# A hybrid recurrent trunk: 21 pairs of projections by seven products ahead of alternating mixers

## The chip, the cores and the metric

The kernel runs on one core of a Trainium2 chip. The metric is the device time of one execution in microseconds. Before the change it is 2498.74 us, the median of three runs (2498.58 to 2500.35). The engines are TensorE (PE, with its weight loads as PEld), VectorE (DVE), ScalarE (ACT), GpSimd (POOL) and SyncE (SP), which only issues DMAs here.

## The reference

One layer over 1024 frames of 1024 channels, all in float32:

```
h = rmsnorm(x, norm1_g)
q, f, i, g | qk, v, if, o | z, xbc, dt | gate = split(h @ w_in)
HGRN2 (8 heads of 128):  y_hg = rmsnorm(scan(silu(q), log forget(f), i)) * silu(g)
mLSTM (4 heads of 128/256): qk = silu(causal_conv4(qk)); y_ml = rmsnorm(scan(qk, v, if)) * sigmoid(o)
Mamba-2 (4 groups):  xBC = silu(causal_conv4(xbc)); y_mb = rmsnorm((scan(xBC, dt) + d*x) * silu(z))
x = x + (sum_b sigmoid(gate_b) * (y_b @ w_br_b)) @ w_out
x = x + (silu(u_g) * u_v) @ w_down,   u = causal_conv3(rmsnorm(x, norm2_g) @ w_up)
out = rmsnorm(x, final_g)
```

The columns of `w_in` come in blocks of 128. The ones that matter here: `w_hg` (forget, query and output gate of each HGRN2 head), `w_ml` (query, key and two output gates of each mLSTM head), `w_mb` (two x blocks, B and C of each Mamba group), `w_gate` (24 blocks of branch gates) and `w_v` (values in token order, in pairs of blocks).

## The kernel before

Channels lie on the 128 partitions and the 1024 frames along the free axis; `h` is kept in two halves of 512 frames, each as a high and a low part in a rounded 32-bit format. Each weight block is loaded on SP's queue into one of four raw buffers (`weight_`, L106 to 113), split into a high part by ACT (L99) and a low part by DVE (L100), and multiplied in three combinations (high by high, high by low, low by high). A plain block (`gemm`, L136) is 8 x 3 x 2 = 48 matmuls of 512 columns into one of two wide PSUM buffers (`ps_g`). A value pair (`gemm_tok`, L274) is 192 matmuls of 256 columns.

A pair of blocks can also be made by seven half-sized products instead of eight (`pair_gemm`, L171): 7 x 4 x 3 = 84 matmuls for two blocks. For it four sums of quarters of `h` are kept as high and low parts (`sums`, tile `t`, eight buffers), and per pair the weights are combined by four subtractions on DVE (L160) and split again; the products are joined by ACT copies (L188, L191) and DVE additions (L183). Its PE order is fixed as written.

Elsewhere a planner orders each engine's instructions from a model of their times: it takes them in the order of the program as far as they are ready, and weight loads with a higher priority. Tiles rotate through a fixed number of buffers (`BUFS`): `v`, `q`, `k`, `b` and `z` have two, `ta` four, `kT`, `C`, `qe` and `num` one, the outer `gate` three.

The stages: `first` makes `h` from the norm (its two halves), and begins the forget and query blocks and the values of the first heads on the half that is ready; the normed halves are also stored to `h_d`. Then come eight HGRN2 heads (three plain blocks each, and a value pair for every two heads; six levels of small products, L468, between DVE and ACT work), the scalars of mLSTM and Mamba after the sixth head (one block, then a long row of small operations, some of it by way of DRAM, `rows`), four mLSTM heads (four plain blocks, a value pair), and four Mamba groups (four plain blocks with a four-tap convolution each, a value pair). After all mixers: four branch gates as plain blocks, beside them the sums from `h_d` fetched again, 16 branch gates as eight pairs, and four plain gates. All branch gates and the mixers' outputs are stored to DRAM from POOL's queue (`keep`) and fetched on SP's (`fetch`) by the branch products, and the output projection and the MLP follow, the latter with 19 pairs of its own.

Of the kernel before, what the change touches and what calls it, by code (L numbers as in the profile page):

```python
# [18 lines left out]
P = 128  # L19
# [28 lines left out]
class Trunk:  # L48
# [266 lines left out]
    def first(self, hp, early):  # L315

        nc, tc, ins = self.nc, self.tc, self.ins
        self.h = [[hp.tile([P, KT, HALF], F32R, name=f"h{hf}{part}", align_bytes=ALIGN) for part in range(2)]
                  for hf in range(2)]
        with tc.tile_pool(name="n1", bufs=2, side="left", reuse_waits="tile") as pool:  # L320
            xs = [pool.tile([P, KT, HALF], F32, name="n_x") for _ in range(2)]
            tmp = lambda: pool.tile([P, HALF], F32, name="n_t", bufs=6)
# [23 lines left out]
            vw = [self.weight_(ins["w_v"][i], [pool.tile([P, 1024], F32R, name=n, align_bytes=ALIGN) for n in ("w_hi", "w_lo")])  # L346
                  for i in range(2)]
# [11 lines left out]
        mp = early()  # L359
        v = mp.tile([P, NC_, 256], F32, name="v")  # L360
        for i, p in enumerate(pv):
            nc.scalar.copy(out=v[:, 2 * i:2 * i + 2], in_=p)
        return mp, begun, v
# [20 lines left out]
    def hg_v(self, mp, pair):  # L384
        v = mp.tile([P, NC_, 256], F32, name="v")

# [5 lines left out]
    def hg_head(self, mp, hd, v, begun=None):  # L392
# [4 lines left out]
        ps = begun[0] if begun else self.gemm(wb[3 * hd], self.rhs_h)  # L397
        f = mp.tile([P, T], F32, name="ta")
        nc.scalar.activation(out=f, in_=ps, func=AF.Sigmoid)
        ps = begun[1] if begun else self.gemm(wb[3 * hd + 1], self.rhs_h)  # L400
# [213 lines left out]
    def ml_head(self, mp, hd):  # L614
# [108 lines left out]
    def mb_group(self, mp, g):  # L723
# [4 lines left out]
        def channel(j, blk, name):  # L728
            ps = self.gemm(wb[4 * g + j], self.rhs_h)
            t = mp.tile([P, T], F32, name=name)  # L730
# [115 lines left out]

    def gate_pairs(self, pool, some):
        for i in self.in_order(some):
            cs = [pool.tile([P, T], F32, name="c", bufs=3) for _ in range(2)]
            self.pair_gemm(pool, [self.ins["w_gate"][i + j] for j in range(2)], cs)  # L850
            for j in range(2):
                self.gate_end(i + j, cs[j])
# [183 lines left out]
GATES = 4  # L1036
PLAIN = 3
# [109 lines left out]
def build(tc, ins, outs, dbg=None):  # L1147
    stages = dbg or dict(hg=8, ml=4, mb=4, rest=True)
    left = dict(side="left", reuse_waits="tile")
    right = dict(side="right", reuse_waits="tile")  # L1150
    with ExitStack() as ctx:
# [3 lines left out]
        t.h_d = t.dr.tile([2, P, KT, HALF], F32, name="h_dram")  # L1155
# [3 lines left out]
        with tc.tile_pool(name="gp", bufs=3, **right) as t.gp:  # L1159
            with tc.tile_pool(name="hp", bufs=1, **right) as hp:  # L1160
                with ExitStack() as ms:
                    late = ms.enter_context(tc.tile_pool(name="late", bufs=1, **right))
                    early = lambda: Mix(ms.enter_context(tc.tile_pool(name="early", bufs=1, **right)), late)
                    mp, begun, v = t.first(hp, early)
                    t.late_consts(late)
                    t.hg_setup()
                    for hd in range(stages["hg"]):
                        if hd and hd % 2 == 0:
                            v = t.hg_v(mp, hd // 2)
                        t.hg_head(mp, hd, v, begun if hd == 0 else None)  # L1170
                        if hd == 5:
                            t.scalars(mp)
                    for hd in range(stages["ml"]):
                        t.ml_head(mp, hd)
                    for g in range(stages["mb"]):
                        t.mb_group(mp, g)
                if not stages["rest"]:
                    return
                t.gates(range(GATES))
                with tc.tile_pool(name="tp", bufs=1, **right) as tp:  # L1180
                    with tc.tile_pool(name="hx", bufs=2, **left) as hx:
                        xs = [hx.tile([P, KT, HALF], F32, name="h_x") for _ in range(2)]
                        for ks, hf in itertools.product((slice(0, KT // 2), slice(KT // 2, KT)), range(2)):
                            t.fetch(xs[hf][:, ks], t.h_d[hf][:, ks])
                        quarter = lambda hf, k0: [[t.h[hf][part][:, k0 + k] for k in range(KT // 2)] for part in range(2)]
# [63 lines left out]
```

## Time and profile before

| | |
|---|---|
| median of three runs | 2498.74 us |
| the profiled execution | 2498.8 us |
| its span | 2497.0 us |
| mean granted clock, share of full | 0.994 |
| PE / PEld busy | 99% / 85% of the span |
| DVE / ACT / POOL busy | 60% / 40% / 2% |
| moved by DMA | 228.63 MB, mean 92 GB/s |

Busy time of PE is modelled from starts of pipelined matmuls, so the distance between starts is what one costs, not its mean duration. A stretch of the span is given by its start and end in us, and the busy time of each engine in it can be set against its length: where PE is busy throughout, another engine's work is hidden.

### The profile page before, as it was taken

The page shows a single profiled execution, that of the slowest core. Times are in us where ns is not written, and L with a number is a line of the kernel's source. Part 1 is how long each engine was busy: PE and PEld are TensorE (multiplying, and loading weights), DVE is VectorE, ACT ScalarE, POOL GpSimd, SP SyncE. Part 2 cuts the span into 40 slices and gives each one's busy share as a digit, 9 for nine tenths or more (in the row PEclk, how much of TensorE's full clock was granted, in tenths as well). Part 3 has the DMA queues.
Part 4 walks back from the last instruction along what each step waited for, and adds up shares of the span by engine and source line. Part 5 has one row for each costly group of instructions (what it writes and reads, how often), then busy time and mean ns, then how long its engine had stood idle before and what let it go on. Part 6 is the DMA issues. An engine that isn't in the chain of part 4 may idle for free.

```text
span 2497.0 us, 31129 instructions
## 1 busy us (share of the span) xinstructions
PE 2464.3 (99%) x12980; PEld 2116.6 (85%) x12980; DVE 1508.2 (60%) x1888; ACT 1005.8 (40%) x1233; POOL 62.2 (2%) x99
## 2 busy tenths in 40 slices
PE   8999999999999999999999999999999999999998
PEld 6898989889988898998888888888878888878886
DVE  6576767873443366756765323354687887875445
ACT  4444445553433263555444312122344544542212
POOL 2000000000000000000000000000000000000000
PEclk8999999999999999999999999999999999999999
DMA  5111010111211122122333454354412222243321
GB/s 218 35 35 51 35 51 26 62 60 43 76 60 60 61 83 76 52 93 80 141 104 109 134 168 169 95 190 134 142 55 91 78 85 85 85 160 128 109 76 68
DMA packets 64141, 228.63 MB, mean 92 GB/s; under 512 B 7400, under 2 KB 8040, under 8 KB 63232
## 3 DMA queue, kind: packets, MB, share of 16 engines
q1 hardware_dynamic: 52352, 181.54, 21.9%
q0 software_dynamic: 11648, 45.09, 4.6%
q8 instruction: 102, 1.67, 0.3%
q14 instruction: 39, 0.32, 0.0%
HBM read 177.23 MB, written 49.38 MB: 91 GB/s over the span
## 4 chain that ended last, share of the span: by engine, by line
PE 96%; DVE 2%; issue 1%; ACT 1%; DMA 0%; SPq 0%; DVEq 0%; ACTq 0%
PE ps_g L136 48%; PE ps_m L171 15%; PE ps_g L274 10%; PE ps_g L171 6%; PE ps_m L136 5%; PE ps_m L468 3%; PE ps_m L801 1%; PE ps_m L274 1%; PE ps_m L477 1%; PE ps_m L712 1%; PE ps_m L683 1%; PE ps_m L487 1%; PE ps_m L440 1%; PE ps_m L663 0%; PE ps_m L685 0%
## 5 line engine op out<-in xcount | busy, mean ns | idle before, releaser
L136 PE MATMUL ps_g<-h,w_hi 128*128 128x512 f32 x2080 | 585.4, 398 | 5.8 <-DVE h L100 3.9
L99 ACT CAST w_hi<-w_raw 128x1024 fp32r<-128x1024 f32 x209 | 218.9, 1048 | 738.9 <-PE ps_g L136 541.0
L136 PEld LDWEIGHTS ps_g<-h,w_hi 128*128 128x128 f32 x2080 | 388.2, 189 | 85.6 <-DVE h L100 4.7
L100 DVE TENSOR_TENSOR w_lo<-w_raw,w_hi 128x1024 fp32r<-128x1024 f32 x209 | 254.9, 1220 | 169.3 <-ACT w_hi L99 167.4
L136 PE MATMUL ps_g<-h,w_lo 128*128 128x512 f32 x1040 | 332.3, 395 | 0.0
L274 PE MATMUL ps_g<-w_hi,h 128*128 128x256 f32 x1408 | 261.1, 284 | 0.0
L136 PE MATMUL ps_g<-p_hi,w_hi 128*128 128x512 f32 x768 | 239.5, 390 | 2.8 <-DVE x L1005 2.2
L136 PE MATMUL ps_g<-p_lo,w_hi 128*128 128x512 f32 x768 | 239.2, 389 | 0.8 <-DVE p_lo L100 0.8
L136 PE MATMUL ps_g<-p_hi,w_lo 128*128 128x512 f32 x768 | 239.4, 389 | 0.0
L136 PEld LDWEIGHTS ps_g<-h,w_lo 128*128 128x128 f32 x1040 | 195.6, 188 | 40.3
L274 PEld LDWEIGHTS ps_g<-w_hi,h 128*128 128x128 f32 x1408 | 221.3, 192 | 0.6
L274 PE MATMUL ps_g<-w_lo,h 128*128 128x256 f32 x704 | 200.1, 284 | 0.0
L136 PEld LDWEIGHTS ps_g<-p_hi,w_hi 128*128 128x128 f32 x768 | 144.0, 188 | 34.0 <-DVE x L1005 2.6
L136 PEld LDWEIGHTS ps_g<-p_lo,w_hi 128*128 128x128 f32 x768 | 144.2, 188 | 31.2 <-DVE p_lo L100 1.1
L136 PEld LDWEIGHTS ps_g<-p_hi,w_lo 128*128 128x128 f32 x768 | 144.1, 188 | 30.2 <-DVE w_lo L100 0.3
L274 PEld LDWEIGHTS ps_g<-w_lo,h 128*128 128x128 f32 x704 | 134.9, 192 | 0.5
L171 PE MATMUL ps_m<-t,w_hi 128*128 128x512 f32 x432 | 133.0, 389 | 0.0
L1005 DVE TENSOR_TENSOR x<-ps_g,x 128x1024 f32<-128x1024 f32 x40 | 49.0, 1225 | 89.3 <-PE ps_g L136 85.6
L609 DVE SCALAR_TENSOR_TENSOR gate<-c,c_vec,gate 128x1023 f32<-128x1023 f32 x76 | 95.9, 1281 | 2.0 <-ACT gate L605 1.3
L171 PEld LDWEIGHTS ps_m<-t,w_hi 128*128 128x128 f32 x432 | 81.1, 188 | 16.8
L188 ACT COPY u<-ps_m 128x512 f32<-128x512 f32 x81 | 47.6, 588 | 117.4 <-PE ps_m L171 117.4
L171 PE MATMUL ps_m<-t,w_lo 128*128 128x512 f32 x216 | 84.1, 390 | 1.5 <-DVE w_lo L100 1.5
(317 smaller groups left out, 3913.9 us busy)
## 6 DMA issues: line engine op xcount, KB each, us to landing
w_raw<-w_up SPq DMA_DIRECT2D x44, 512.0 KB, 3.3
w_raw<-w_hg SPq DMA_DIRECT2D x24, 512.0 KB, 3.3
w_raw<-w_v SPq DMA_DIRECT2D x24, 512.0 KB, 3.3
ta<-rows SPq DMA_DIRECT2D x24, 512.0 KB, 4.3
w_raw<-w_gate SPq DMA_DIRECT2D x24, 512.0 KB, 3.5
w_raw<-w_br SPq DMA_DIRECT2D x24, 512.0 KB, 4.3
w_raw<-y_dram SPq DMA_DIRECT2D x24, 512.0 KB, 4.0
gate<-gate_dram SPq DMA_DIRECT2D x24, 512.0 KB, 4.3
```

The lines of the kernel that those rows point to most:

```text
L99: self.nc.scalar.copy(out=hi, in_=src)
L100: (eng or self.nc.vector).tensor_tensor(out=lo, in0=src, in1=hi.bitcast(F32), op=ALU.subtract)
L136: self.nc.tensor.matmul(out=out, lhsT=w[:, ks], rhs=rhs(part, kt, ts), start=kt == 0 and w is hi and part == 0, stop=kt == kts - 1 and w i ...
L171: self.nc.tensor.matmul(out=out, lhsT=w[x][:, ks], rhs=b[y][k], start=start and k == i == 0, stop=stop and k == 3 and i == 2, skip_group_c ...
L188: nc.scalar.copy(out=u[-1], in_=x)
L274: self.nc.tensor.matmul(out=out, lhsT=self.h[hf][part][:, 4 * i + k, o:o + P], rhs=w[:, ks], start=start and k == 0 and w is hi and part = ...
L440: nc.tensor.matmul(out=pu[:, j], lhsT=kdT[:, c], rhs=v[:, c, vs], start=True, stop=True)
L468: nc.tensor.matmul(out=pa[0:m, c], lhsT=z[:, c * P:c * P + m], rhs=part(1)[:, c], start=True, stop=True)
L477: nc.tensor.matmul(out=pa[:, j], lhsT=c3(k)[:, c + j], rhs=qs[:, c + j], start=True, stop=True)
L487: nc.tensor.matmul(out=po[:, j], lhsT=A[:, c], rhs=v[:, c, vs], start=True, stop=c == 0)
L609: end = nc.vector.scalar_tensor_tensor(out=out[:, a:ts.stop], in0=ps[:, a - d:ts.stop - d], scalar=w(d), in1=out[:, a:ts.stop], op0=ALU.mu ...
L1005: nc.vector.tensor_tensor(out=x2[j], in0=ps, in1=x2[j], op=ALU.add)
```

## The change

- `first` begins the branch gates 0 and 1 instead of the first head's forget and query blocks, no longer stores `h`, and makes the sums right after the second half of the norm; the weights of the first value pair lie in two of the `t` buffers meanwhile. The first and the second value pair are both made here and stored (`v_d`). The norm has three temporaries instead of six.
- `projections` then makes 21 pairs by seven products: four of HGRN2 output gates, four of mLSTM output gates, four of mLSTM queries and keys with convolution (`FIRST = 1`), nine of the branch gates 2 to 19. Each result is activated and stored (`g_d`, `c_d`, `gate_d`). The last four branch gates stay plain, after the mixers.
- HGRN2 heads fetch their output gate (and the first four their values); mLSTM heads fetch query, key and output gates. Mamba groups are as before.
- The mixers alternate (`MIXERS`: H an HGRN2 head, L an mLSTM head, G a Mamba group), and the scalars come after the second head.

```
-    def first(self, hp, early):
+    def first(self, hp, tp):
...
-            tmp = lambda: pool.tile([P, HALF], F32, name="n_t", bufs=6)
+            tmp = lambda: pool.tile([P, HALF], F32, name="n_t", bufs=3)
...
-                self.keep(self.h_d[hf], xs[hf])
...
-            ws = [self.weight_(ins["w_hg"][j]) for j in range(2)]
+            ws = [self.weight_(ins["w_gate"][j]) for j in range(2)]
...
+            t3 = [tp.tile([P, KT // 2, HALF], F32R, name="t", align_bytes=ALIGN, bufs=8) for _ in range(2)]
+            flat = [t.rearrange("p k t -> p (k t)") for t in t3]
+            vw = [self.weight_(ins["w_v"][i], [f[:, i * 1024:(i + 1) * 1024] for f in flat]) for i in range(2)]
...
+            self.bs = [quarter(0, 0), quarter(0, KT // 2), quarter(1, KT // 2)] + self.sums(tp, xs)
+            v = [self.gp.tile([P, T], F32, name="gate", bufs=3) for _ in range(2)]
...
+            self.gemm_tok(ins["w_v"][2:4], evac)
+
+    def projections(self, pool):
+        nc, ins = self.nc, self.ins
+        plain, conv = [], []
+        for hd in range(0, 8, 2):
+            plain.append([(ins["w_hg"][3 * h + 2], self.g_d[h], AF.Silu) for h in (hd, hd + 1)])
+        for hd in range(4):
+            b = 4 * hd
+            plain.append([(ins["w_ml"][b + 2 + j], self.g_d[8 + 2 * hd + j], AF.Sigmoid) for j in range(2)])
+            if FIRST > 0:
+                conv.append([(ins["w_ml"][b + j], self.c_d[2 * hd + j], "ml_conv", 4 * j + hd) for j in range(2)])
...
+        for b in range(2, 24 - GATES, 2):
+            plain.append([(ins["w_gate"][i], self.gate_d[i], AF.Sigmoid) for i in (b, b + 1)])
+        jobs, at = [], 0
+        for i, p in enumerate(plain):
+            jobs.append(p)
+            if (i + 1) * len(conv) // len(plain) > at:
+                jobs.append(conv[at])
+                at += 1
+        for job in self.in_order(jobs):
+            cs = [pool.tile([P, T], F32, name="c", bufs=3) for _ in job]
+            self.pair_gemm(pool, [j[0] for j in job], cs)
+            for c, (_, dst, *how) in zip(cs, job):
+                g = c
+                if len(how) == 2:
+                    g = self.gp.tile([P, T], F32, name="gate", bufs=3)
+                    self.conv(g, c, *how, 4)
+                nc.scalar.activation(out=g, in_=g, func=AF.Silu if len(how) == 2 else how[0])
+                self.keep(dst, g)
...
     def hg_v(self, mp, pair):
+        if pair < 2:
+            for i in range(2):
+                self.fetch(v[:, 4 * i:4 * i + 4], self.v_d[pair, i].rearrange("p (c x) -> p c x", x=256))
+            return v
...
     def hg_head(self, mp, hd, v):
-        ps = self.gemm(wb[3 * hd + 2], self.rhs_h)
         g = self.gp.tile([P, T], F32, name="gate", bufs=3)
-        nc.scalar.copy(out=g, in_=ps)
-        nc.scalar.activation(out=g, in_=g, func=AF.Silu)
+        self.fetch(g, self.g_d[hd])
...
     def ml_head(self, mp, hd):
+            t = mp.tile([P, T], F32, name="qk"[j])
+            if FIRST > 0:
+                self.fetch(t, self.c_d[2 * hd + j])
+                continue
...
-            ps = self.gemm(wb[4 * hd + 2 + j], self.rhs_h)
             g = self.gp.tile([P, T], F32, name="gate", bufs=3)
-            nc.scalar.activation(out=g, in_=ps, func=AF.Sigmoid)
+            self.fetch(g, self.g_d[8 + 2 * hd + j])
...
+GATES = 4
+FIRST = 1
+MIXERS = "HHLHHGHHLHHGLGLG"
...
+                with tc.tile_pool(name="tp", bufs=1, **right) as tp:
+                    t.first(hp, tp)
+                    with tc.tile_pool(name="a1", bufs=1, **left) as pool:
+                        t.projections(pool)
...
+                    for kind in MIXERS:
+                        n = at[kind]
+                        at[kind] += 1
+                        if kind == "H":
+                            if n % 2 == 0:
+                                v = t.hg_v(mp, n // 2)
+                            t.hg_head(mp, n, v)
+                            if n == 1:
+                                t.scalars(mp)
+                        elif kind == "L":
+                            t.ml_head(mp, n)
+                        else:
+                            t.mb_group(mp, n)
```

## Rows read from the trace of the kernel before

**Rows 1.** the page: span, busy time by engine, the chain that ended last
```profile
span 2497.0 us, 31129 instructions
...
PE 2464.3 (99%) x12980; PEld 2116.6 (85%) x12980; DVE 1508.2 (60%) x1888; ACT 1005.8 (40%) x1233; POOL 62.2 (2%) x99
...
PE 96%; DVE 2%; issue 1%; ACT 1%; DMA 0%; SPq 0%; DVEq 0%; ACTq 0%
PE ps_g L136 48%; PE ps_m L171 15%; PE ps_g L274 10%; PE ps_g L171 6%; PE ps_m L136 5%; PE ps_m L468 3%; PE ps_m L801 1%; PE ps_m L274 1%; PE ps_m L477 1%; PE ps_m L712 1%; PE ps_m L683 1%; PE ps_m L487 1%; PE ps_m L440 1%; PE ps_m L663 0%; PE ps_m L685 0%
```

**Rows 2.** the chain in order of time: start us, us, what
```profile
62.14 10.55 PE ps_m L274 x88
...
590.46 21.78 PE ps_g L136 x96
646.30 11.51 PE ps_g L274 x96
```

**Rows 3.** the PE timeline, two starts of a pair: start us, us, what
```profile
1277.01 0.62 PE L171 MATMUL ps_m<-h,w_hi 128*128 128x512 f32 x2
...
1296.05 0.62 PE L171 MATMUL ps_m<-h,w_hi 128*128 128x512 f32 x2
```

**Rows 4.** busy time by stretch; the header names the columns
```profile
core 0: us, PE busy (x) PEld busy (x) DVE busy (x) ACT busy (x) POOL busy (x), PEclk, DMA share, GB/s
191.40:317.12 125.72, 125.72 (x823) 113.60 (x823) 85.89 (x142) 57.57 (x60) 1.07 (x2) 1.00 0.13 43
378.74:519.41 140.67, 138.98 (x887) 124.12 (x887) 108.67 (x183) 74.69 (x76) 2.98 (x4) 1.00 0.13 43
671.10:751.77 80.67, 80.67 (x468) 71.64 (x468) 32.92 (x39) 28.38 (x38) 1.07 (x2) 1.00 0.19 66
981.10:1067.20 86.10, 86.10 (x534) 77.59 (x533) 56.72 (x69) 43.19 (x70) 1.07 (x2) 1.00 0.22 74
1277.01:1296.05 19.04, 19.04 (x86) 15.77 (x84) 9.91 (x12) 8.04 (x11) 1.11 (x3) 1.00 0.36 111
251.79:308.40 56.61, 56.61 (x435) 53.83 (x434) 42.26 (x71) 26.84 (x29) 0.53 (x1) 1.00 0.11 38
```

**Rows 5.** groups by form: count, busy us, mean ns, idle time before and its releasers
```profile
L100 DVE TENSOR_TENSOR w_lo<-w_raw,w_hi 128x1024 fp32r<-128x1024 f32 x209 | 254.9, 1220 | 169.3 <-ACT w_hi L99 167.4
...
L99 ACT CAST w_hi<-w_raw 128x1024 fp32r<-128x1024 f32 x209 | 218.9, 1048 | 738.9 <-PE ps_g L136 541.0 <-PE ps_m L171 47.7 <-issue 47.7
...
L609 DVE SCALAR_TENSOR_TENSOR gate<-c,c_vec,gate 128x1023 f32<-128x1023 f32 x38 | 48.7, 1281 | 1.3 <-ACT gate L605 1.3
...
L605 ACT ACTIVATE gate<-c,c_vec 128x1024 f32<-128x1024 f32 x38 | 47.4, 1248 | 3.5 <-DVE c L183 2.9
```

**Rows 6.** the DVE timeline where the sums are made: start us, us, what
```profile
1233.15 2.35 DVE L225 TENSOR_TENSOR h_x<-h_x 128x1024 f32<-128x1024 f32 x2
...
1237.29 6.90 DVE L225 TENSOR_TENSOR h_x<-h_x 128x1024 f32<-128x1024 f32 x6 [0.65 <-DMA h_x<-h_dram]
...
1250.70 5.76 DVE L100 TENSOR_TENSOR t<-h_x,t 128x1024 fp32r<-128x1024 f32 x5
```

**Rows 7.** busy time by stretch, of the start
```profile
8.00:18.00 10.00, 3.94 (x10) 2.28 (x10) 9.08 (x18) 8.96 (x16) 0.00 (x0) 0.69 1.03 418
18.00:24.00 6.00, 1.22 (x2) 0.50 (x2) 6.00 (x11) 5.73 (x11) 2.14 (x3) 0.50 0.68 260
24.00:28.50 4.50, 4.44 (x11) 3.47 (x12) 4.50 (x8) 1.57 (x3) 4.50 (x1) 0.50 0.99 408
```

**Rows 8.** DMA issues: KB each, median us from issue to landing
```profile
w_raw<-w_hg SPq DMA_DIRECT2D x24, 512.0 KB, 3.3
...
ta<-rows SPq DMA_DIRECT2D x24, 512.0 KB, 4.3
```

**Rows 9.** waits of SP's queue: us in total, times, longest us
```profile
engine line waited for: us in total, times, longest us
SPq L108 <- DVE w_lo L100: 1281.5, 129, 30.4
...
SPq L598 <- PE ps_m L739: 83.8, 8, 12.1
```

**Rows 10.** the PE timeline around one level of an HGRN2 head
```profile
219.30 0.96 PE L136 MATMUL ps_g<-h,w_hi 128*128 128x512 f32 x3
...
228.28 0.62 PE L136 MATMUL ps_g<-h,w_lo 128*128 128x512 f32 x2
228.74 3.46 PE L468 MATMUL ps_m<-z 128*128 128x64 f32 x30
```

**Rows 11.** the DVE timeline around the same level
```profile
225.16 0.69 DVE L464 TENSOR_TENSOR z<-z,q 128x512 f32<-128x512 f32 x1
...
230.67 0.71 DVE L521 COPY_PREDICATED hgA<-c_hmask,ps_m 128x512 f32<-128x512 uint8 x1 [3.69 <-PE ps_m L468]
```

More of the change, by code (lines that the diff above doesn't have):

```diff
@@ L358, in first @@
                 self.tok_tile(vw, c, pv[c // 2][:, c % 2])
[L359 to L363, printed above, removed]
+            quarter = lambda hf, k0: [[self.h[hf][part][:, k0 + k] for k in range(KT // 2)] for part in range(2)]
+            self.bs = [quarter(0, 0), quarter(0, KT // 2), quarter(1, KT // 2)] + self.sums(tp, xs)
+            v = [self.gp.tile([P, T], F32, name="gate", bufs=3) for _ in range(2)]
@@ new lines, in first, with evac @@
+            for i, p in enumerate(pv):
+                nc.scalar.copy(out=v[i // 2][:, (i % 2) * HALF:(i % 2 + 1) * HALF], in_=p.rearrange("p c x -> p (c x)"))
+            for i in range(2):
+                self.keep(self.v_d[0, i], v[i])
+            for i in range(2):
+                g = self.gp.tile([P, T], F32, name="gate", bufs=3)
+                nc.scalar.activation(out=g, in_=begun[i], func=AF.Sigmoid)
+                self.keep(self.gate_d[i], g)
+            def evac(cs, ps):
+                g = self.gp.tile([P, T], F32, name="gate", bufs=3)
+                nc.scalar.copy(out=g, in_=ps.rearrange("p c x -> p (c x)"))
+                self.keep(self.v_d[1, cs.start // 4], g)
@@ new lines, in first @@
+            self.gemm_tok(ins["w_v"][2:4], evac)
[9 more added lines that the diff above has]
+                conv.append([(ins["w_ml"][b + j], self.c_d[2 * hd + j], "ml_conv", 4 * j + hd) for j in range(2)])
+        for g in range(4 if FIRST > 1 else 0):
+            b = 4 * g
+            for js in ((2, 3), (0, 1)):
+                conv.append([(ins["w_mb"][b + j], self.c_d[8 + b + j], "mb_conv", (2 * g, 2 * g + 1, 8 + g, 12 + g)[j])
+                             for j in js])
+        for b in range(2, 24 - GATES, 2):
[12 more added lines that the diff above has]
+                if len(how) == 2:
+                    g = self.gp.tile([P, T], F32, name="gate", bufs=3)
+                    self.conv(g, c, *how, 4)
+                nc.scalar.activation(out=g, in_=g, func=AF.Silu if len(how) == 2 else how[0])
+                self.keep(dst, g)
@@ L385, in hg_v @@
         v = mp.tile([P, NC_, 256], F32, name="v")
+        if pair < 2:
+            for i in range(2):
+                self.fetch(v[:, 4 * i:4 * i + 4], self.v_d[pair, i].rearrange("p (c x) -> p c x", x=256))
+            return v
         def evac(cs, ps):
@@ L390, in hg_v, with hg_head @@
         return v
-    def hg_head(self, mp, hd, v, begun=None):
+    def hg_head(self, mp, hd, v):
         nc = self.nc
@@ L728, in channel @@
         def channel(j, blk, name):
+            t = mp.tile([P, T], F32, name=name)
+            if FIRST > 1:
+                self.fetch(t, self.c_d[8 + 4 * g + j])
+                return t
             ps = self.gemm(wb[4 * g + j], self.rhs_h)
-            t = mp.tile([P, T], F32, name=name)
             self.conv(t, ps, "mb_conv", blk, 4)
@@ L845, in gates @@
             self.keep(self.gate_d[i], g)
[L847 to L852, printed above, removed]
     def gate(self, i):
@@ L1154, in build @@
             t.dr.tile([KT, P, T], F32, name=f"y_dram{i}") for i in range(3)]
-        t.h_d = t.dr.tile([2, P, KT, HALF], F32, name="h_dram")
+        t.v_d = t.dr.tile([2, 2, P, T], F32, name="v_dram")
+        t.g_d = t.dr.tile([16, P, T], F32, name="g_dram")
+        t.c_d = t.dr.tile([24, P, T], F32, name="c_dram")
         t.gate_d = t.dr.tile([24, P, T], F32, name="gate_dram")
@@ L1164, in build @@
-                    mp, begun, v = t.first(hp, early)
+                    mp = Mix(ms.enter_context(tc.tile_pool(name="early", bufs=1, **right)), late)
                     t.late_consts(late)
                     t.hg_setup()
[L1167 to L1185, printed above, removed]
-                        t.bs = [quarter(0, 0), quarter(0, KT // 2), quarter(1, KT // 2)] + t.sums(tp, xs)
-                    with tc.tile_pool(name="a1", bufs=1, **left) as pool:
-                        t.gate_pairs(pool, range(GATES, 24 - GATES, 2))
+                    at = dict(H=0, L=0, G=0)
```

18 lines of the change are left out of this document (5 added, 13 removed).

## The prediction

> **What bounds the kernel now.** I read the page first [rows 1]: TensorE (PE) is busy for 2464.3 of the 2497.0 us span, and 96% of the chain that ended last is PE. So before the change only two things move the end: fewer or shorter matmuls, or new time in which PE has nothing to do. The profiled execution took 2498.8 us, 1.8 us beyond its span; the median of the timed runs is 2498.74 us, so the sum below is made against 2498.8 and needs no correction.
>
> Then the chain in order of time, for prices of PE work [rows 2]: 96 matmuls of 512 columns take 21.78 us, so a plain block of 48 takes 10.89; 96 token matmuls of 256 columns take 11.51, so a value pair of 192 takes 23.02. The PE timeline of two pairs by seven products [rows 3] shows the same matmul 19.04 us apart (1277.01 and 1296.05), which is the price of a pair; two plain blocks are 21.78.
>
> Last, busy time by stage [rows 4]. In a stretch of two HGRN2 heads (191.40 to 317.12) PE is busy for all 125.72 us and VectorE (DVE) for 85.89. One mLSTM head is 80.67 with 32.92 of DVE, one Mamba group 86.10 with 56.72. The reader is to see that PE never waits in the mixers because each head brings plain blocks that fill its pauses. These are what the change takes out.
>
> **The change part by part.**
>
> *Blocks to pairs.* 26 plain blocks go: 8 output gates of HGRN2, 16 blocks of mLSTM (queries, keys, two output gates for four heads), and net two branch gates (8 plain before, 6 after). They become 13 further pairs (21 instead of 8). 26 x 10.89 = 283.1 less 13 x 19.04 = 247.5: 35.6 us less PE work. The value products of heads 2 and 3 move forward at the same price. Without any new wait: 2498.8 - 35.6 = 2463.2.
>
> *Do the pairs still run at 19.04?* One pair occupies 9.91 us of DVE and 8.04 of ScalarE (ACT) in its 19.04 [rows 4]. A convolved pair adds two blocks of three taps, 6 x 1.28 = 7.7 of DVE, and two of 1.25 on ACT [rows 5]: 17.6 of 19.04, with three or four plain pairs between convolved ones. Yes: nothing added.
>
> *The sums move to the front.* Before, they stood beside plain gates: from 1233.15 to 1256.46 DVE made the eight differences and eight low parts [rows 6]. Now they follow the second half of the norm. They hide behind the last token products (10.55 us for 88 [rows 2]) and the value pair moved forward (23.02), 33 us for about 23 us of work, plus weight splits. Two high/low tiles first lend their space to weights and are free only when those products end. Bounds 0 and 10; I take 2. The norm's three temporaries instead of six cost nothing I can see: from 8 to 18 us the DMA engines are full [rows 7].
>
> *The stores and fetches.* 28 loads of 512 KB come into the mixers, on SP's queue. Behind a fetch that waits for its buffer stand all later weight loads, and a late weight would cost landing, cast and low part, 3.3 + 1.05 + 1.22 = 5.6 us of PE [rows 5, 8]. Bounds: 0, and 16 mixers x 5.6 = 90. The nearest row is the fetch of the `rows` tile, 24 times at 4.3 us: SP waited 83.8 us at that line for PE's transposes [rows 9], and PE lost nothing. SP mostly waits for a raw weight buffer (1281.5 us), so it is ahead. I take 0. The stores are on POOL's queue, with nothing urgent behind them.
>
> *The mixers with less filler.* This decides. Small matmuls of an HGRN2 head: (125.72 - 6 x 10.89 - 23.02) / 2 = 18.7 us. After the change a head is 2 x 10.89 + 18.7 = 40.5 of PE; its DVE, without the weight splits that left, is (85.89 - 4 x 1.22) / 2 = 40.5 where the values are fetched too. So PE and DVE are exactly level in the first four heads. In the last four each couple of heads keeps a value pair: 103.9 against 83.4. An mLSTM head is 80.67 - 43.56 = 37.1 of PE; DVE 32.92 less four splits and six taps = 20.4. Mamba stays 86.1 and 56.7. The scalars take about 15 of PE and 22.8 of DVE (the stretch from 378.74 less two heads [rows 4]).
>
> Totals: PE 877, DVE 660 over the mixers. Where PE waits is seen in the order HHL, HHG, HHL, HHG, LG, LG.
>
> First HHL: DVE starts when the first forget block is done and passed through ACT, about 12.5 us; then 81.0 + 22.8 + 20.4 = 124.2; and gaps. In one head's chain before (251.79 to 308.40) DVE stood for 56.61 - 42.26 = 14.3 us [rows 4]. Much of that is PE's own order: the last input of eight products was ready at 225.85, PE went on with plain blocks until 228.74, and DVE waited 3.69 [rows 10, 11]. With less filler I take a third, 5 per head and for L: 152 in all. PE has 2 x 40.5 + 15 + 37.1 = 133 of its own, and the two wide PSUM buffers let it make the next head's two blocks, 21.8: 155. Idle 0 to 10, taken 3.
>
> First HHG: the next head's forget tile needs one of the four `ta` buffers, which mLSTM holds until its weights are multiplied in; about 4 us of DVE are lost there. The heads need 81.0 + 10 + 4 = 95 on DVE; PE has 80.9 - 21.8 already made + two Mamba blocks ahead (21.8, into `k` and `q`) = 80.9: 14 idle. Then Mamba, 86 on PE against 62: none.
>
> Second HHL and HHG: 103.9 against 93.4: none. LG, LG: none. At the end four plain gates (43.6) still cover the last Mamba group, as eight did.
>
> Sum: 2463.2 + 2 + 3 + 14 = 2482.2 us. The bounds for the idle time: 0, and what the third rival gives, about 55.
>
> *A rule against the change.* The start shows what idle time can do besides: from 8 to 18 us PE was busy 3.94 of 10, and then the granted clock was 0.50, the lower level of 1.2 GHz, from 18 to 28.5; once PE was kept busy it rose [rows 7]. The Trainium skill (TensorE: Matmul & The Clock Gate, Why this matters for your kernels) says that a pause between bursts of matmuls puts the array back to half its clock, and asks for loops without such pauses. By the rows the clock stays 1.00 through all mixers of before, where there are no pauses; by the rule it may fall where I expect 17 us of idle time. My sum has it at 1.00, since those are many short waits between small products; the other case is the fourth rival.
>
> **The rivals.**
> 1. *Idle time as above*, 8 to 32 us: 2471 to 2495, likeliest 2482. Chance 0.50.
> 2. *The cover holds*: alternation lends PE of Mamba and mLSTM to the heads, as DVE's 660 of 877 allows and as zero idle at 68% DVE (85.89 of 125.72) speaks for. Against: the level couples. 2463 to 2471, 2466. Chance 0.15.
> 3. *The heads run at their own chain*, slower than before. Place: HGRN2 heads between Mamba and mLSTM. If a head keeps 56.6 us from forget gate to norm and heads overlap no better, the first four take 226.4 against 161.8 (+64.6), less 43.6 of blocks made ahead; the last four 2 x (113.2 - 103.9) = 18.6; the scalars' chain stands alone for 15: about 55. 2463.2 + 2 + 55 = 2520. It cancels the gain from 35.6 us of idle time, or 49 us per head in the first four. For it: one buffer each of `kT`, `C`, `qe`, `num`, and scalars that use `kT` and `qe` right between a head and the mLSTM head that needs their rows back from DRAM. Against: the gaps were largely PE's order. Chance 0.28, of which 0.08 ends within 5 us of before.
> 4. *The clock falls in the mixers*: 4.5 us at half clock per fall as from 24 to 28.5, 2.25 lost, at eight heads: +18 on my sum, 2500. For it the start; against it the mixers of before. Chance 0.07.
>
> **How the numbers follow.** A difference of 0.2%, 5 us, is about what a measurement can tell. Faster: all of 2 and nearly all of 1, 0.63. Within: 0.02 of 1, 0.08 of 3, 0.04 of 4: 0.14. Slower: 0.20 of 3 and 0.03 of 4: 0.23. Predicted 2482. The range: 2462, the sum without a wait, to 2514, where most of rival 3 is inside and little more than one in ten lies above.
>
> **What would show it.** Right: pairs 19.04 apart from about 95 to 495 us, granted clock 1.00, PE idle time of some 15 to 20 us nearly all between 495 and 800 us before L468, L477, L487 or the mLSTM's products, released by DVE, and none after. Wrong: idle time in the pairs (DVE or the sums are late); PE waiting for w_hi behind a fetch on SP; a busy share of DVE above 90% across the first heads and still long PE waits (rival 3 with dense DVE), or DVE below 80% there with both engines waiting for each other (rival 3 as a chain); a clock below 1.00 in the mixers (rival 4). The forecast as a whole fails if the mixers take over 912 us, or under 880.

## The result and the profile after

The changed kernel takes 2543.86 us (median; 2543.03 to 2544.73) against 2498.66 of the kernel before on the same chip. The ratio is 1.0179 [1.0162 to 1.0197]: 1.8% slower, where 2482 was forecast. The profiled execution took 2543.09 us; its mean granted clock is 0.982, against 0.994 before.

From the page: the span, busy times by engine, the PE slices and the granted clock by slice, the shares of the chain that ended last.

```profile
span 2541.3 us, 31194 instructions
...
PE 2454.9 (97%) x12824; PEld 2107.4 (83%) x12824; DVE 1600.8 (63%) x2018; ACT 1035.1 (41%) x1291; POOL 76.8 (3%) x125
...
PE   8999999999788999998999999999999999999997
...
PEclk8999999999889999999999999999999999999998
...
PE 91%; DVE 6%; ACT 2%; issue 1%; DMA 0%; DVEq 0%; ACTq 0%
```

Against [rows 1], PE is busy for only 9.4 us less, not 35.6, and PE has fallen from 96% to 91% of the chain. PE dips in slices 11 to 13 and 19 of the 40 (63.5 us each); the granted clock falls to 0.8 in slices 11 and 12.

The chain in order of time, two pairs by seven products at the front (start us, us, what):

```profile
100.79 8.16 PE ps_m L171 x36
...
119.83 8.16 PE ps_m L171 x36
```

They stand 19.04 us apart, as in [rows 3].

Busy time by stretch (the header names the columns):

```profile
core 0: us, PE busy (x) PEld busy (x) DVE busy (x) ACT busy (x) POOL busy (x), PEclk, DMA share, GB/s
95.33:467.20 371.87, 371.87 (x1642) 307.88 (x1642) 213.68 (x253) 174.02 (x209) 20.79 (x39) 1.00 0.33 111
486.00:640.00 154.00, 147.06 (x911) 129.87 (x909) 115.18 (x188) 74.43 (x78) 4.46 (x6) 1.00 0.24 81
640.00:810.00 170.00, 137.95 (x747) 121.02 (x748) 121.92 (x191) 75.23 (x94) 2.13 (x4) 0.87 0.15 51
715.00:718.00 3.00, 3.00 (x28) 2.98 (x27) 2.75 (x4) 0.22 (x1) 0.00 (x0) 1.00 0.21 41
718.10:721.43 3.33, 0.02 (x1) 0.03 (x1) 3.33 (x7) 2.12 (x2) 0.00 (x0) 1.00 0.32 119
721.43:728.12 6.69, 6.69 (x33) 6.69 (x34) 1.85 (x3) 0.00 (x0) 0.00 (x0) 0.53 0.01 2
728.12:732.00 3.88, 3.88 (x14) 3.88 (x14) 3.06 (x5) 0.00 (x0) 0.00 (x0) 0.50 0.00 0
810.00:1030.00 220.00, 220.00 (x1579) 206.62 (x1578) 134.74 (x217) 85.30 (x119) 2.68 (x5) 1.00 0.21 70
1030.00:1170.00 140.00, 122.04 (x710) 106.50 (x709) 109.01 (x164) 71.82 (x84) 1.60 (x3) 0.94 0.17 57
1170.00:1515.00 345.00, 345.00 (x2184) 313.63 (x2183) 205.39 (x262) 156.96 (x247) 8.00 (x15) 1.00 0.32 107
```

The front, up to 467, is as forecast: PE busy in every us, clock 1.00. So are the first Mamba group with the two heads after it (810 to 1030) and all from the second Mamba group on (1170). The loss lies from 486 to 810 (the first HHL and the two heads after it) and from 1030 to 1170 (the second mLSTM head and the last two HGRN2 heads). From 640 to 810 PE is idle for 32 of 170 us and the clock is 0.87, while DVE, at 121.92 of 170 (72%), is not full either.

The PE timeline, the largest of those pauses and one undisturbed product (start us, us, line, what; in brackets the idle time before it and what ended it):

```profile
642.05 1.94 PE L640 MATMUL ps_m<-c_ident,kT 128*128 128x128 f32 x8 [5.82 <-DVE kT L623]
...
680.15 2.08 PE L136 MATMUL ps_g<-h,w_hi 128*128 128x512 f32 x4 [7.86 <-ACT ta L451]
...
714.43 3.68 PE L518 MATMUL ps_m<-z 128*128 128x64 f32 x32
...
721.43 6.69 PE L518 MATMUL ps_m<-z 128*128 128x64 f32 x32 [3.31 <-DVE z L514]
...
752.02 1.45 PE L764 MATMUL ps_m<-c_ident,num 128*128 128x128 f32 x8 [3.47 <-DVE num L543]
...
804.40 0.55 PE L274 MATMUL ps_g<-w_hi,h 128*128 128x256 f32 x1 [9.02 <-DVE r L552]
...
1162.57 0.55 PE L274 MATMUL ps_g<-w_hi,h 128*128 128x256 f32 x1 [9.03 <-DVE r L552]
```

Between 490 and 1520 us the idle times of PE add up to 56.7 us (3.2 before, from 95 to 1600 us), and PE is busy for 46.3 us at half clock. The same 32 matmuls take 3.68 us at 1.00 and 6.69 at a mean of 0.53 (714.43 and 721.43 above); half of the 46.3, 23.1 us, is taken as lost. An account: 2463.2 (the forecast's sum with no new wait) + 56.7 - 3.2 + 23.1 = 2539.8; measured 2543.1 in that execution. About 3 us stay open in it. Over the whole span the trace closes it: idle time of PE grew by 53.7 us (86.4 against 32.7) and the loss by half clock by 24.0 (29.9 against 6.0), and PE's busy time without that loss fell by 33.4 us, some 2 less than forecast.

The wait of 7.86 at 680.15 is for the sigmoid of the next head's forget gate. PE's last matmuls of a plain block before it, and ACT's timeline there:

```profile
665.16 0.63 PE L136 MATMUL ps_g<-h,w_lo 128*128 128x512 f32 x2
```

```profile
675.76 2.00 ACT L749 ACTIVATE ta<-num 128x1024 f32<-128x1024 f32 x2 [3.06 <-DVE num L745]
677.78 1.28 ACT L451 ACT_TABLE_LOAD   x1
679.08 1.02 ACT L451 ACTIVATE ta<-ps_g 128x1024 f32<-128x1024 f32 x1
680.12 1.28 ACT L751 ACT_TABLE_LOAD   x1
```

The block that the sigmoid (L451) reads was complete by 665.8 at the latest. On ACT the sigmoid stands behind the squares of the mLSTM tail (L749), and these wait for DVE, which can begin that tail only at 672.7, when ACT has copied the last product of the mLSTM head (L738). The waits of 9.02 are the same thing on PSUM: both wide buffers hold Mamba blocks whose taps (L659, DVE) stand among the last steps of the head before, and PE may make nothing further until one is read. (The profile names the step of DVE next to the last tap, L552.)

### The profile page after: what moved, and what is told of

Same layout as the page of the kernel before. It is cut to its first block, busy times and chain, and to the rows that moved or that the text cites. A ratio compares the mean times of both kernels' runs of the same rounds, so it can differ in the third digit from the quotient of the medians.

```text
span 2541.3 us, 31194 instructions
## 1 busy us (share of the span) xinstructions
PE 2454.9 (97%) x12824; PEld 2107.4 (83%) x12824; DVE 1600.8 (63%) x2018; ACT 1035.1 (41%) x1291; POOL 76.8 (3%) x125
## 4 chain that ended last, share of the span: by engine, by line
PE 91%; DVE 6%; ACT 2%; issue 1%; DMA 0%; DVEq 0%; ACTq 0%
PE ps_g L136 34%; PE ps_m L171 21%; PE ps_g L274 10%; PE ps_g L171 9%; PE ps_m L136 5%; PE ps_m L518 3%; PE ps_m L856 1%; PE ps_m L527 1%; PE ps_m L274 1%; PE ps_m L764 1%; PE ps_m L735 1%; PE ps_m L715 0%; PE ps_m L737 0%; PE ps_m L840 0%; PE ps_m L827 0%
## 5 line engine op out<-in xcount | busy, mean ns | idle before, releaser
L136 PE MATMUL ps_g<-h,w_hi 128*128 128x512 f32 x1248 | 357.7, 401 | 21.3 <-ACT ta L451 12.1
L136 PEld LDWEIGHTS ps_g<-h,w_hi 128*128 128x128 f32 x1248 | 235.7, 191 | 73.0 <-ACT ta L451 13.3
L136 PE MATMUL ps_g<-h,w_lo 128*128 128x512 f32 x624 | 202.3, 398 | 0.0
L171 PE MATMUL ps_m<-t,w_hi 128*128 128x512 f32 x640 | 197.0, 389 | 0.0
L171 PEld LDWEIGHTS ps_m<-t,w_hi 128*128 128x128 f32 x640 | 120.1, 188 | 24.9
L136 PEld LDWEIGHTS ps_g<-h,w_lo 128*128 128x128 f32 x624 | 118.4, 190 | 24.5
L183 DVE TENSOR_TENSOR c<-ps_g,u 128x512 f32<-128x512 f32 x80 | 55.2, 690 | 130.8 <-PE ps_g L171 130.8
L188 ACT COPY u<-ps_m 128x512 f32<-128x512 f32 x120 | 70.5, 587 | 161.6 <-PE ps_m L171 161.6
L659 DVE SCALAR_TENSOR_TENSOR gate<-c,c_vec,gate 128x1023 f32<-128x1023 f32 (+2 forms) x100 | 125.8, 1280 | 5.7 <-ACT gate L655 5.0
L171 PE MATMUL ps_m<-t,w_lo 128*128 128x512 f32 x320 | 124.5, 389 | 0.0
```

What stands on the lines that cost most here:

```text
L136: self.nc.tensor.matmul(out=out, lhsT=w[:, ks], rhs=rhs(part, kt, ts), start=kt == 0 and w is hi and part == 0, stop=kt == kts - 1 and w i ...
L171: self.nc.tensor.matmul(out=out, lhsT=w[x][:, ks], rhs=b[y][k], start=start and k == i == 0, stop=stop and k == 3 and i == 2, skip_group_c ...
L183: add = lambda out, p, q: nc.vector.tensor_tensor(out=out, in0=p, in1=q, op=ALU.add)
L188: nc.scalar.copy(out=u[-1], in_=x)
L659: end = nc.vector.scalar_tensor_tensor(out=out[:, a:ts.stop], in0=ps[:, a - d:ts.stop - d], scalar=w(d), in1=out[:, a:ts.stop], op0=ALU.mu ...
```

## The experiments

**Theories.** *Cover:* a head keeps a chain of its own between DVE, ACT and PE that is longer than the work PE has left; the blocks that were taken away were its cover. *Order:* the alternation HHLHHG, in which unlike mixers meet, makes the waits. *Buffers:* a held buffer (`ta`, or one of the two `z`) sets the head's pace. *Seam:* each wait has its own local cause and goes with it.

Of every run the same account can be made. "No-wait" is 2498.8 less the PE work that its pairs save (a pair for two plain blocks saves 2.74); idle and clock loss are read as above in the profiled execution, from the first mixer on; the sum is no-wait + idle - 3.2 + clock loss, and beside it stands the median of all runs.

| run | no-wait | idle | clock loss | sum | measured |
|---|---|---|---|---|---|
| changed kernel | 2463.2 | 56.7 | 23.1 | 2539.8 | 2543.9 |
| a: output gates in the heads | 2474.1 | 23.2 | 10.3 | 2504.4 | 2504.3 |
| b: queries, keys in the heads | 2474.1 | 51.3 | 21.1 | 2543.3 | 2544.6 |
| c: heads first, L, then G | 2463.2 | 45.4 | 16.7 | 2522.1 | 2523.8 |
| e: fifth `ta` | 2463.2 | 58.7 | 22.1 | 2540.8 | 2545.9 |
| x: Mamba values first | 2463.2 | 56.3 | 26.5 | 2542.8 | 2547.6 |
| g: heads in a row, with gates | 2474.1 | 10.7 | 1.7 | 2483.3 | 2484.1 |
| h: heads in a row | 2463.2 | 51.5 | 22.7 | 2534.2 | 2536.3 |
| k: g, Mamba's blocks in front | 2452.2 | 38.0 | 10.5 | 2497.5 | 2501.5 |
| q: g, two gates at the end | 2471.4 | 12.5 | 0 | 2480.7 | 2482.8 |
| m: g, late heads' gates in front | 2468.7 | 43.5 | 14.4 | 2523.4 | 2524.5 |
| n: h, third `z` | 2463.2 | 39.1 | 4.3 | 2503.4 | 2507.0 |
| p: g, third `z` | 2474.1 | 2.2 | 0 | 2473.1 | 2474.3 |
| s: m, third `z` | 2468.7 | 22.7 | 3.5 | 2491.7 | 2494.4 |
| r: changed, third `z` | 2463.2 | 31.9 | 9.0 | 2500.9 | 2503.6 |
| t: a, third `z` | 2474.1 | 9.2 | 0 | 2480.1 | 2481.1 |

All agree within 6 us, so what a version costs is read off its two middle columns.

**a and b. Undo one half of the new pairs each.** a puts the output gates back into the heads as plain blocks (17 pairs), b the mLSTM's queries and keys.

```diff
-        for hd in range(0, 8, 2):
-            plain.append([(ins["w_hg"][3 * h + 2], self.g_d[h], AF.Silu) for h in (hd, hd + 1)])
...
+        ps = self.gemm(wb[3 * hd + 2], self.rhs_h)
...
-        self.fetch(g, self.g_d[hd])
+        nc.scalar.copy(out=g, in_=ps)
+        nc.scalar.activation(out=g, in_=g, func=AF.Silu)
```
```diff
-FIRST = 1
+FIRST = 0
```

> The eight HGRN2 output gates go back into their heads as plain blocks; 17 pairs are left in front, the alternating order stays. Without any wait this is 2463.2 + 4 x 2.74 = 2474 us. Theory (the blocks that left the heads were the cover of their DVE and ACT chains, and each wait of PE that is left open also lets the clock fall): a head has 51.4 us of PE again against 41.7 of DVE, so most of the 57 us of idle time and 23 us of half clock go: 2485 to 2515 us, clock above 0.99. Rival (the alternating order itself costs the time, whatever fills it): both stay, about 2554 us.

> The mLSTM queries and keys go back into their heads as plain blocks with their convolution; 17 pairs in front, the alternating order stays. Without any wait 2474 us, as with the HGRN2 gates back. Theory (cover): the same 87 us of PE work, but in the heads that have little DVE work, so only the waits beside an mLSTM head go (some 18 us of idle time and 6 of half clock of the 80): about 2530 us, clearly slower than with the HGRN2 gates back. Rival (order): 2554. Rival (any 87 us of filler helps alike): the same as with the HGRN2 gates back.

a: 2504.26, ratio 1.0022 [1.0012 to 1.0031]; 8 blocks of 10.89 put back won 39.6 us. b: 2544.63, 1.0186 [1.0170 to 1.0201], nothing, a miss: its four mLSTM heads got their blocks back, but a new wait of 12.88 us for a tap appeared. It is the cover inside the HGRN2 heads that matters.

**c. The old grouping of mixers.** All eight heads, then L, then G.

```diff
-MIXERS = "HHLHHGHHLHHGLGLG"
+MIXERS = "HHHHHHHHLLLLGGGG"
...
-                            if n == 1:
+                            if n == 5:
```

> All 21 pairs stay in front, but the mixers come in the order of before: eight HGRN2 heads, four mLSTM heads, four Mamba groups, with the scalars after the sixth head. Without any wait 2463 us. Theory (cover): eight heads in a row have 40.5 of PE against 40.5 of DVE (four of them 51.9), and four mLSTM heads in a row 37 of PE against a chain of some 45: more waits than with alternation, 2550 to 2580 us. Rival (the alternating order costs the time): 2463 to 2490 us.

2523.84, 1.0104 [1.0089 to 1.0119], below what cover gave and far above what order gave: both missed. The order of the mixers makes some 20 of the 80 us that lie between no-wait and measured; 60 stay without it.

**e and x. Two local causes.** e gives the mixers a fifth `ta` (the step of the prediction by which the mLSTM holds the next head's buffer); x moves Mamba's value product, whose wide PSUM buffers are read by ACT and not by taps on DVE, ahead of its `x` blocks (the same lines, taken from below them).

```diff
-z=2, ta=4
+z=2, ta=5
```
```diff
+        z = [self.gp.tile([P, 4, 256], F32, name="gate", bufs=3) for _ in range(2)]
+        def evac(cs, ps):
+            nc.scalar.activation(out=z[cs.start // 4], in_=ps, func=AF.Silu)
+        self.gemm_tok(self.ins["w_v"][16 + 2 * g:18 + 2 * g], evac)
...
```

> The changed kernel with five ta buffers instead of four, so that the forget tile of the head behind an mLSTM head need not wait for one. Theory (cover): that wait is one of several places where PE runs out of what it may do ahead; its 7.9 and 2.3 us (680 and 698 us) shrink and come back in part behind the next one: 2532 to 2546 us. Rival (the ta buffer is the cause): these waits, the one at 1036 us and the half clock behind them go, some 12 us idle and 6 of clock: 2526 us or less.

> The changed kernel with the Mamba group's value product (23 us of PE, passed on by ACT) ahead of its two x blocks (passed on by convolutions on DVE, behind the HGRN2 head's work there). Theory for the two waits of 9.0 us (804 and 1162 us): both wide PSUM buffers hold x blocks whose taps stand behind the head on DVE; with the value product in between they are read in time, and the two waits and the half clock behind them (some 5 us) go: about 2520 us. Rival (PE has simply run out of work there, so the wait comes back at another place): 2535 to 2545.

e: 2545.92, 1.0189 [1.0174 to 1.0204]. The wait of 7.86 stays (7.87 there): it is not the buffer, and that step of the prediction falls; by the timeline above it is ACT's order. x: 2547.59, 1.0192 [1.0178 to 1.0206], where its theory had 2520 and its rival 2535 to 2545. The waits of 9.02 are gone, and as much came elsewhere; from x's PE timeline:

```profile
1073.06 7.06 PE L518 MATMUL ps_m<-z 128*128 128x64 f32 x32 [5.04 <-DVE z L514]
...
1423.99 2.07 PE L136 MATMUL ps_g<-h,w_hi 128*128 128x512 f32 x4 [4.41 <-ACT gate L802]
```

So at these two places *seam* falls as well: one buffer more gained nothing, and with the other wait gone PE only ran out of work at another place.

**g, h, k, q. Heads in a row, scalars after the sixth, L and G alternating.** g has the output gates in the heads (17 pairs), h has them in front (21 pairs); k is g with all four convolved blocks of each Mamba group in front too (25 pairs); q is g with two more branch gates in front, so that two are left for the end. g, k and q have the edit of a besides the lines shown.

```diff
-MIXERS = "HHLHHGHHLHHGLGLG"
+MIXERS = "HHHHHHHHLGLGLGLG"
...
-                            if n == 1:
+                            if n == 5:
```
```diff
-FIRST = 1
+FIRST = 2    # k
-GATES = 4
+GATES = 2    # q
```

> Eight HGRN2 heads in a row with their output gates as plain blocks in them, then mLSTM heads and Mamba groups in turn (L, G four times), scalars after the sixth head; 17 pairs in front. Without any wait 2474 us. Theory (the heads need their own third block as cover; mLSTM heads, which have little DVE work, need only a Mamba group next to them): heads have 51 to 63 of PE against 42 of DVE as before, and the turn of mLSTM and Mamba had no idle time in the changed kernel (1200 to 1550 us): 2474 to 2486, faster than before. Rival (any head that loses blocks, or any alternation, costs waits): 2500 or more.

> The same order, but with all 21 pairs in front, so that the heads fetch their output gates. Without any wait 2463 us. Theory: the heads in a row are level in PE and DVE and wait as they did in the run with the old order (some 20 us of idle time up to 890 us, and 8 to 10 of half clock), the rest is clean: 2488 to 2498, slower than with the gates in the heads although it has 11 us less PE work. Rival (the waits came from the places where mLSTM and Mamba met the heads): 2463 to 2474.

> As the run with heads in a row and their gates in them, but the 16 convolved Mamba blocks also go to the front: 25 pairs. Without any wait 2474 - 8 x 2.74 = 2452 us. The turn of an mLSTM head and a Mamba group then has 37 + 42.5 of PE against 20 + 36 of DVE. Theory (cover, 71% of DVE there): some waits, 10 to 20 us with their half clock: 2462 to 2474. Rival (the Mamba group's plain blocks are all the cover that the mLSTM head has): 2485 or more.

> g_heads_row_gates with two plain branch gates at the end instead of four: 18 pairs, without any wait 2471 us. Theory: two blocks (21.8 us) and the first branch products cover the tail of the last Mamba group as well: 2479 to 2483. Rival (the tail needs the 43.6 us): 2487 or more.

g: 2484.06, 0.9939 [0.9925 to 0.9953], as expected. h: 2536.30, 1.0148 [1.0133 to 1.0162], a miss: 10.9 us less PE work than g, and 52 us slower. This pair alone shows that the gates were cover, and h shows the pace of a head, since its heads stand side by side. The row of heads with the scalars, and the place where it meets the first mLSTM (the seam), with the columns of the busy times by stretch above:

```profile
498.50:940.00 441.50, 417.11 (x2678) 374.64 (x2676) 333.56 (x566) 211.95 (x218) 6.68 (x11) 0.97 0.17 59
940.00:1045.00 105.00, 77.91 (x438) 70.30 (x438) 67.10 (x91) 41.30 (x66) 1.60 (x3) 0.82 0.21 75
```

PE idles for 24.4 us in the row and for 27.1 at the seam. The outputs of the heads are stored at 579.81, 632.42, 689.75, 745.21 and 799.85, 55.0 us a head. Busy time between the first and the last of these (same columns):

```profile
579.81:799.85 220.04, 203.75 (x1340) 185.69 (x1339) 162.57 (x278) 98.05 (x101) 2.13 (x5) 0.95 0.13 44
```

DVE works 162.57 / 4 = 40.6 us a head, the forecast's 40.5. The other 14.4 it stands, and the 14.3 of before [rows 4] are all still there. What it stands for, on DVE and then on PE:

```profile
705.15 0.69 DVE L510 TENSOR_TENSOR z<-b 128x512 f32<-128x512 f32 x1
...
710.75 0.68 DVE L514 TENSOR_TENSOR z<-z,q 128x512 f32<-128x512 f32 x1
716.15 0.70 DVE L571 COPY_PREDICATED hgA<-c_hmask,ps_m 128x512 f32<-128x512 uint8 x1 [4.71 <-PE ps_m L518]
```

```profile
702.43 3.68 PE L518 MATMUL ps_m<-z 128*128 128x64 f32 x32
...
713.75 0.62 PE L136 MATMUL ps_g<-h,w_lo 128*128 128x512 f32 x2
...
714.21 3.68 PE L518 MATMUL ps_m<-z 128*128 128x64 f32 x32
...
1030.79 3.65 PE L764 MATMUL ps_m<-c_ident,num 128*128 128x128 f32 x16 [16.12 <-DVE num L753]
```

With two `z` buffers, DVE can begin the `z` of the head's last two levels only while PE makes the products of the two levels before (702.43): it begins at 705.15 and has them ready at 711.4. Its next step is to read their products, so it waits; PE runs the plain block that stands ahead in its order until 714.21, and then the products take 3.68. In turn PE has no cover left when DVE makes the next `z`. Such waits of DVE for the products of a level add up to 24.9 of the 57.5 us that it stands in these four heads. The wait of 16.12 is at the seam.

k: 2501.46, 1.0010 [1.0000 to 1.0019], a miss by 27 (its rival, that these blocks are all the cover that the mLSTM heads have, had 2485 or more): 21.9 us of PE work saved and more than that lost. The waits are at the tail of the mLSTM heads, whose cover Mamba's blocks had been:

```profile
1209.15 3.65 PE L764 MATMUL ps_m<-c_ident,num 128*128 128x128 f32 x16 [7.09 <-DVE num L753]
...
1395.10 3.65 PE L764 MATMUL ps_m<-c_ident,num 128*128 128x128 f32 x16 [9.95 <-DVE num L753]
```

q: 2482.81, 0.9936 [0.9920 to 0.9953], as expected: with two plain gates less at the end, no wait came of it there.

**m, n, p, s. How much cover, and the third `z`.** m is h with the gates of heads 0 to 3 inside (19 pairs); n, p and s are h, g and m with one buffer more for the level's `z`.

```diff
-        for hd in range(0, 8, 2):
+        for hd in range(4, 8, 2):    # m, s
...
+        if hd < 4:
+            ps = self.gemm(wb[3 * hd + 2], self.rhs_h)
```
```diff
-z=2
+z=3    # n, p, s
```

> As g_heads_row_gates, but only the first four heads make their output gate themselves; the last four, which have a value product in every second head, fetch it: 19 pairs. Without any wait 2474 - 2 x 2.74 = 2469 us. Theory (a head takes about 55 us whatever PE has beside it: outputs of heads were stored 52 to 57 us apart in h_heads_row and 56 to 61 in g_heads_row_gates; it is that chain, not the 41 us of DVE busy time, that PE must be kept busy for): with 51.9 of PE in each of the last four heads PE waits 15 to 30 us and runs 5 to 10 more at half clock: 2490 to 2508, slower than g_heads_row_gates (2484). Rival (busy time decides: 52 of PE against 42 of DVE is cover enough): 2470 to 2482.

> h_heads_row (all 21 pairs in front) with three z buffers instead of two, so that a third level of an HGRN2 head can be begun while two are on ACT and PE. If the head's 55 us come from its levels handing two tiles round DVE, ACT and PE: 2505 to 2522. If they come from the order in which the instructions stand on PE and DVE, or from the front and end of a head: 2530 to 2542, as before (2536).

> g_heads_row_gates with three z buffers. There PE waits only 10.7 us in all, so a shorter chain of the heads can give little: 2478 to 2486, within 0.2% of 2484.

> m_late_gates_front (19 pairs, 2524) with a third z buffer. Without any wait 2469. If the shorter chain of the heads makes their 51.9 us of PE cover enough: 2469 to 2478, better than p_heads_row_gates_z3. If the seam from the last head to the first mLSTM head keeps its waits (7.7 and 16.1 us there, which a third buffer did not shrink with all pairs in front): 2490 to 2505.

m: 2524.50, 1.0103 [1.0088 to 1.0119], a miss, worse than expected. Its row of heads and its seam:

```profile
460.00:930.00 470.00, 453.52 (x2887) 404.38 (x2886) 340.23 (x574) 228.31 (x233) 6.69 (x11) 0.99 0.17 56
930.00:1035.00 105.00, 77.91 (x444) 70.31 (x443) 68.86 (x91) 42.50 (x68) 1.60 (x3) 0.84 0.21 73
```

In the row PE idles for 16.5 us, as was expected of it: the value pairs of the last four heads (11.5 us a head) are not cover enough, 40.5 + 11.5 = 52 of PE against a pace of 55. The excess is the seam, 27.1 us as in h, which the expectation left out. n: 2507.03, 1.0033 [1.0020 to 1.0047], 29 us below h. Its stores lie 49.3 us apart (583.40 to 780.43, four heads):

```profile
583.40:780.43 197.03, 190.88 (x1347) 175.24 (x1346) 159.57 (x276) 93.97 (x99) 2.12 (x4) 1.00 0.14 49
```

DVE now stands 9.4 us a head instead of 14.4, and the clock is back at 1.00. PE is busy for 190.88 of the 197.03 us, so 49.3 is no longer the pace of the chain alone. What DVE waited for in h and in n, in those four heads (us in total, times, longest):

```profile
DVE hgA L571 <- PE ps_m L518: 24.9, 9, 4.7
```

```profile
DVE hgA L571 <- PE ps_m L518: 11.0, 9, 4.1
```

Of the 20.0 us less that DVE stands, 13.9 are this wait for the products of a level, the one that hands a `z` buffer on. What is left lies mostly at the seam, which the third `z` hardly changed (24.2 us of idle time, 27.1 in h); in the row of heads 24.4 became 14.9:

```profile
499.90:910.00 410.10, 395.23 (x2635) 356.51 (x2635) 332.43 (x567) 212.35 (x218) 6.70 (x11) 1.00 0.18 61
910.00:1015.00 105.00, 80.80 (x489) 72.15 (x488) 67.02 (x90) 41.89 (x67) 1.60 (x3) 0.89 0.24 83
```

```profile
1000.31 3.65 PE L764 MATMUL ps_m<-c_ident,num 128*128 128x128 f32 x16 [16.12 <-DVE num L753]
```

p: 2474.29, 0.9902 [0.9887 to 0.9916], the fastest, 24 us below the kernel before and 4 below the range expected (2478 to 2486), a miss to the good side: of the 10.7 us of idle time and 1.7 of clock in g, 2.2 and nothing are left. Page and stretches of its mixers:

```profile
span 2471.9 us, 31175 instructions
...
PE 2441.5 (99%) x12872; PEld 2098.1 (85%) x12872; DVE 1570.8 (64%) x1978; ACT 1043.9 (42%) x1289; POOL 72.5 (3%) x117
```

```profile
410.00:700.00 290.00, 288.73 (x1758) 254.58 (x1757) 209.37 (x350) 155.54 (x157) 4.15 (x7) 1.00 0.15 52
700.00:980.00 280.00, 279.06 (x1789) 251.50 (x1788) 204.57 (x319) 133.60 (x159) 5.10 (x8) 1.00 0.20 67
980.00:1450.00 470.00, 470.00 (x2987) 427.92 (x2987) 283.26 (x361) 219.32 (x346) 9.59 (x18) 1.00 0.30 101
```

PE idles for 2.2 us in 1040, and the time is the no-wait sum. s: 2494.36, 0.9980 [0.9971 to 0.9990]; 15.33 of its 22.7 us of idle time is one wait, at the seam:

```profile
987.80 3.65 PE L770 MATMUL ps_m<-c_ident,num 128*128 128x128 f32 x16 [15.33 <-DVE num L759]
```

**r and t. The third `z` in the alternating order.** r is the changed kernel with it, t is a with it.

> The changed kernel itself with a third z buffer. Without any wait 2463. If the levels' two z buffers are the whole cause of its 80 us: 2465 to 2485. If the places where the mixers meet are as much of it (642 to 698 us at the scalars and the mLSTM head, 804 and 1162 us at the Mamba groups: 36 of the 57 us of idle time, and their half clock): only the waits inside the heads go, and 2515 to 2530 is left.

> The alternating order with the HGRN2 gates in their heads (a_hg_gates_in_heads, 2504) and a third z buffer. Without any wait 2474. If the third buffer frees the heads of their waits here as it did in a row (p_heads_row_gates_z3, 2474.3): 2474 to 2482, and the alternating order as such costs nothing. If the meeting places cost by themselves (9.0 us before the Mamba group at 750 us, 3.9 at 635): 2488 to 2500.

r: 2503.56, 1.0018 [1.0009 to 1.0028]: half of the loss, 40 of 80 us, goes with one more `z`. It lies between the two cases expected. The meeting of mLSTM and head keeps its wait, the taps' shrank:

```profile
677.77 2.07 PE L136 MATMUL ps_g<-h,w_hi 128*128 128x512 f32 x4 [7.86 <-ACT ta L451]
...
788.39 0.36 PE L274 MATMUL ps_g<-w_hi,h 128*128 128x256 f32 x1 [1.49 <-DVE ta L659]
```

t: 2481.14, 0.9926 [0.9909 to 0.9943]. The alternation costs 7 us against p once the heads have cover and a third `z`; *order* costs little by itself.

## Why the prediction was wrong

*Right:* the price of a pair (19.04) and, within some 2 us, the 35.6 us of PE work. PE's busy time fell by 9.4, although 24.0 more of it is now the cost of half clock: 33.4. p shows the same price with no waits left. The three-tap blocks hide in the pairs, the sums cost nothing (taken 2), the fetches on SP release no wait of PE, and the heads' 40.5 of DVE was measured as 40.6.

*Wrong, the step that decides:* "With less filler I take a third, 5 per head". The gap of 14.3 was read as an effect of PE's plain blocks that would go with them. It stayed 14.4. A third of that belongs to the two `z` buffers (9.4 are left with a third one), and a part to small products queued behind whatever plain block is left (the 4.71 above); the rest was not taken apart. With 55.0 us a head instead of about 46, PE idles. Rival 3 had named this (56.6 a head, and as a chain: "both engines waiting for each other"), and priced its idle time at 55; measured were 56.7 - 3.2 = 53.5; its sign, DVE below 80%, came too (72%). Its 2520 lacks only the clock, but that the sum fits so well is in part luck: the two waits of 9.02 for Mamba's taps were not in it, and the single buffers that it argued from (`kT`, `C`, `qe`, `num`) were not tested. Its "49 us per head" leaves out the 43.6 us of blocks made ahead that its own sum takes off.

*Wrong, the place:* "none after" 800. The second HHL and HHG were taken as covered, 103.9 of PE against 93.4 of DVE; the stretch from 1030 to 1170 lost 18.0 us of idle time. Busy time against busy time says nothing where the gap is 14 a head; the 16.5 us in m's row of heads show it again. "taken 3" and "14 idle" were 56.7 in all.

*Wrong, the cause:* the four us for a held `ta`; e shows that it is no buffer, and ACT's timeline shows what stands ahead.

*Wrong, the clock:* "My sum has it at 1.00". The fourth rival had the mechanism and priced it at 18, eight falls at 2.25; in the trace it is nine falls and 23.1, on top of the third and not instead of it. The undisturbed product at 714.43 takes 3.68; after 3.31 us of idle time the same 32 take 6.69, at 0.53. The Trainium skill (TensorE: Matmul & The Clock Gate, Why this matters for your kernels) warns of pauses of PE between bursts of matmuls, because one that is long enough puts it back to half clock; the trace agrees with it at 721.43, though not after every pause of such a length: q has one of 3.50 us and nothing at half clock in its mixers. By that rule the clock would have had a term in the sum, where the forecast has nothing.

*Open:* the wait of 15 to 16 us at the first mLSTM tail after a row of heads (c, h, m, n, s; not in g and p) was not taken apart, nor what is left in r around the scalars and the first mLSTM head (16.7 us of idle time from 635 to 700 us). Every edit also lets the planner order the instructions anew, and the order on DVE and ACT differs between h and n, so the gain of the third `z` is that of the buffer and its order together. Nor was an order tried in which a level's products stand ahead of the plain block, or the next head's sigmoid ahead of the mLSTM's squares.

## What to carry to other kernels

A block of matmuls that fills another stage's pauses is worth its price only if it is cheaper elsewhere by more than the cover that it gives: ask first what pace the stage keeps by itself, read as the distance between two of its outputs, not as its busy time. A pause in that stage belongs to what makes it (here in part two rotating buffers and an instruction order), not to the work that happens to lie in it. Here leaving the gates in the heads, with the heads in a row and one more buffer for the chain, gave 1% (p), where moving all 21 pairs out in alternating order cost 1.8%.

## What the runs showed of the hardware

In the changed kernel idle time of PE cost four tenths as much again: with 56.7 us of pauses came 46.3 us of matmuls at half clock, which lost 23.1. In the other versions the share ran from nothing (p, q, t) to 0.47 (x), so it is no fixed price. A pause of 3.3 us was followed by a fall: PE was busy at 1.00 from 715 to 718, idle for 3.3 us, and was then granted 0.53 and 0.50 (the lower level of 1.2 GHz) until 732, though busy throughout. And of the 7.86 us that PE waited at 680.15, 2.3 are a sigmoid of 1.02 and the table load of 1.28 before it; right behind the sigmoid the square root of the other mixer (L751) has a load of 1.28 of its own.
